# PEER's expert sums in a two-layer decoder trunk: v's rows as the moving operand, 512 channels at a time

## The chip, the cores and the metric

The kernel runs on one core of one Trainium2 chip. Its time is device microseconds (us) of one execution. The kernel before takes 2011.32 us, the median of three runs (2011.18 to 2011.91). The engines are TensorE (PE; its weight loads are listed as PEld), VectorE (DVE), ScalarE (ACT), GpSimd (POOL) and SyncE (SP, which issues the DMAs). All of them work side by side, each through its own instructions in order, and wait for one another by semaphores.

## The reference

Two layers of a decoder trunk work on 256 tokens of 1024 channels in float32. Each layer has a mixer (layer 0: mLSTM and block attention, layer 1: differential attention) and then PEER, a feed-forward part that retrieves experts:

```python
def peer_ffn(x, wq, keys, u, v):            # x: 256 tokens x 1024
    qry = (xt @ wq).reshape(t, PEER_HEADS, 2, PEER_DK // 2)
    sub = einsum('thpd,pnd->thpn', qry, keys)        # 8 heads, 2 x 128 sub-keys
    s_top, i_top = lax.top_k(sub, 16)
    ...                                              # 16 best of the 256 candidates
    idx, gate = ...                                  # out of 128 * 128 experts, softmax gates
    act = gelu(einsum('td,thkd->thk', x, u[idx])) * gate
    return einsum('thk,thkd->td', act, v[idx])       # added to x, times a gate of the layer
```

The last line is what the change is about: for every token a gated sum of rows of v, which has 16384 rows of 1024 channels.

## The kernel before

The kernel does not gather. It computes PEER densely: the 16384 experts are 128 tiles of 128. In the first half of `peer_body` it forms for each tile the 128 x 256 values gelu(u x) (`h_tile`) and multiplies them by a gate that is zero where the expert was not chosen (`gate_group`); the results stay in SBUF as A, 128 experts on the partitions by 256 tokens, 128 times. In the second half (the loop over `order`, lines 889 to 929) it sums A times v over all experts.

Products have float32 accuracy by splitting. Each operand is cast to a rounded part `hi` (float32r) and the rest `lo`; three matmuls, hi x hi, hi x lo and lo x hi, stand for one product. For a tile of v, `wsplit` has SP load 128 x 1024 floats (512 KB) into a ring of buffers `raw`, ACT cast it to `hi` (line 159) and DVE subtract to `lo` (line 162); `hi` and `lo` have three buffers each, so these two run up to three tiles ahead of PE. For each group of four tiles ACT and DVE split A in the same way into `act` (lines 904 and 905, two buffers, of the tag "x" in the pool `hp`). Beside it, `side` loads rows of the next modulation matrix, which DVE reduces (line 252): in layer 0, 8 steps over the first 64 tiles and 24 over the next 52; in layer 1, 8 late ones. From tile 64 on the ring `raw` is 15 buffers deep, before that 3.

The sums of the second half stand with channels on the partitions: `acc[dt]`, 128 channels by 256 tokens, for eight `dt`. A block of v (128 experts x 128 channels) is the stationary operand and A (128 experts x 256 tokens) the moving one, so a tile takes 8 x 3 matmuls of 256 columns. The eight sums lie in six PSUM banks: dt 0 to 3 share two of the tag "acc" in pairs, dt 4 and 5 have one each of that tag, and dt 6 and 7 one each of the tag "h". As two sums share a bank, the banks are first cleared by a matmul with zeros (line 891) and all matmuls add. At the last tile (the last three tiles are taken together, `batch`) each finished sum goes to `ffn_out`: DVE multiplies it by the gate and adds it to xT, the residual stream (line 935). In layer 0 `norm_stat` follows, where ACT squares and DVE adds for the next norm, and after the eighth PE sums over the partitions (line 290) with some matmuls of zeros around it (line 268); in layer 1 SP sends each 128 channels out (line 939).

Instructions are recorded in program order and then put in order for each engine by a scheduler that looks at dependences and priorities, so neighbours in the code can change places on an engine.

Another stage of the kernel has matmuls of 512 columns: `mm_row` (lines 237 to 239), in which the activations are stationary and 512 columns of a weight move, again in three products.

Of the kernel before, what the change touches and what calls it, by code (L numbers as in the profile page):

```python
# [9 lines left out]
F32 = mybir.dt.float32  # L10
# [10 lines left out]
P = 128  # L21
D = 1024
KD = D // P
T = 256
TT = T // P
EPS = 1e-6
NEG = -1e32
NEXP = 128
# [27 lines left out]
class Cols:  # L56
# [14 lines left out]
    c = 174  # L71
# [3 lines left out]
class Prog:  # L75
# [743 lines left out]
    def peer_body(self, layer, side, st):  # L819
        nc, tc = self.nc, self.tc  # L820
# [4 lines left out]
        hp = self.hp  # L825
# [11 lines left out]
        h = (hhi, hlo)  # L837
# [9 lines left out]
        for i, ps in self.col_tiles([self.io["wq"][layer, i] for i in range(16)], h, ("acc",) * 3, ws=ws):  # L847
            q = sp.tile([P, T], F32, tag="qry", name="qry", bufs=2)
# [14 lines left out]
        while live:  # L863
# [6 lines left out]
            with tc.issue_after(self.last_lo.ins):  # L870
                while credit > 0 and live:
                    c = next(topk, None)
# [7 lines left out]
        while i < NEXP:  # L880
# [5 lines left out]
                ohs = nxt  # L886
                done += G_TOK
            yield
        banks = [self.psum("acc") for _ in range(4)] + [self.psum("h") for _ in range(2)]
        for b in banks:  # L890
            nc.tensor.matmul(b, lhsT=self.zero.to_broadcast([P, P]), rhs=self.iota.unsqueeze(1).to_broadcast([P, 4, P]),
                             start=True, stop=False)
        acc = [banks[k // 2 if k < 4 else k - 2][:, k % 2 * T if k < 4 else 0:][:, :T] for k in range(KD)]
        order = list(range(64, 128)) + list(range(64))
        batch, nside = [], 0
        for n, e in enumerate(order):
            if n % 4 == 0:
                if n == 64:
                    a1p.__exit__(None, None, None)
                    late = st.enter_context(tc.tile_pool(name=f"late{layer}", bufs=1, reuse_waits="tile"))  # L900
                    self.raw_ring = (late, LATE_RING)
                x = hp.tile([P, 2, 4, T], F32, tag="x", name="act")
                src = A[e // 64][:, e % 64:e % 64 + 4, :]
                nc.scalar.copy(x[:, 0].bitcast(F32R), src)  # L904
                nc.vector.tensor_tensor(out=x[:, 1].bitcast(F32R), in0=src, in1=x[:, 0], op=ALU.subtract)  # L905
                xr = x.bitcast(F32R)
            vhi, vlo = self.wsplit(v[e])
            while nside < SIDE_N[layer][0] * min(n, 64) / 64 + SIDE_N[layer][1] * max(n - 64, 0) / SIDE_P2:
                next(side, None)
                nside += 1  # L910
            if n == NEXP - 8:
                for _ in side:
                    pass
            batch.append((n, vhi, vlo, xr))
            if n < NEXP - 3 or n == NEXP - 1:
                for dt in range(KD):
                    for m, vhi, vlo, xr in batch:
                        s = slice(dt * P, (dt + 1) * P)
                        xhi, xlo = xr[:, 0, m % 4, :], xr[:, 1, m % 4, :]
                        nc.tensor.matmul(acc[dt], lhsT=vhi[:, s], rhs=xhi, start=False, stop=False)  # L920
                        nc.tensor.matmul(acc[dt], lhsT=vhi[:, s], rhs=xlo, start=False, stop=False)  # L921
                        nc.tensor.matmul(acc[dt], lhsT=vlo[:, s], rhs=xhi, start=False, stop=m == NEXP - 1 and dt not in (0, 2))  # L922
                    if n == NEXP - 1 and dt not in (0, 2):
                        for d in (dt - 1, dt) if dt < 4 else (dt,):
                            self.ffn_out(layer, d, acc[d])
                batch = []
            yield
        self.raw_ring = self.stream_ring
        yield

    def ffn_out(self, layer, kd, y):

        nc = self.nc
        x = self.xT[:, kd, :]
        nc.vector.scalar_tensor_tensor(x, y, self.mod[:, layer, 40 + kd:41 + kd], x, op0=ALU.mult, op1=ALU.add)
        if layer == 0:
            self.norm_stat(kd)
        else:
            nc.sync.dma_start(self.out[:, kd, :], x)
# [263 lines left out]
```

## Time and profile before

| | |
|---|---|
| median of three runs | 2011.32 us |
| the profiled execution's own time | 2012.58 us |
| its span in the trace | 2010.8 us |
| PE busy | 1970.7 us (98%) |
| DVE, ACT busy | 1536.1 us (76%), 1131.6 us (56%) |
| second half of PEER, layer 0 | about 650 to 1020 us |
| second half of PEER, layer 1 | about 1636 to 2007 us |

All rows come from one profiled execution. A matmul's row gives its start and how long it was under way; matmuls overlap, so what one costs in a row of them is the distance between starts, not that duration. "PEclk" is the granted clock of TensorE as a share of its full 2.4 GHz. "DMA share" is the mean busy share of the core's 16 DMA engines. An idle time before an instruction is given in brackets with what ended it.

### The profile page before, as it was taken

Reading aid. Unit: us, or ns where it says so; the run is one execution under the profiler, and the core shown is the slowest. Engines: PE = TensorE matmul, PEld = TensorE weight load, DVE = VectorE, ACT = ScalarE, POOL = GpSimd, SP = SyncE. Lnnn points to the kernel's source line nnn. Section 1 sums busy time; section 2 is a strip of 40 time slices with the busy share of each in tenths; the row PEclk is TensorE's granted clock in tenths of the full one; section 3 lists DMA queues with packets and bytes.
Section 4 is the critical chain, followed back from the end, with each engine's and each line's share of the span. In section 5 each row is a group of like instructions: output and inputs, shape, how many; then the busy total and the mean of one; then the engine's idle time right before and its main releaser. Section 6 shows DMA issues by size and latency. Waiting matters only on the chain.

```text
span 2010.8 us, 41035 instructions
## 1 busy us (share of the span) xinstructions
PE 1970.7 (98%) x16281; PEld 1912.6 (95%) x16281; DVE 1536.1 (76%) x3328; ACT 1131.6 (56%) x2129; POOL 48.3 (2%) x37
## 2 busy tenths in 40 slices
PE   5999999999999999999999999999999999999999
PEld 4888999999999999999988799999999999999999
DVE  8887998788998555677578789988899955556554
ACT  4655555878775444444456554567877644444443
POOL 0020000000000000000012100000000000000000
PEclk9999999999999999999999999999999999999999
DMA  8863355444445666998266143554444455569650
GB/s 325 283 211 128 108 183 187 158 164 162 154 158 189 195 210 204 339 320 305 84 226 206 62 150 116 179 178 162 164 158 158 158 180 186 181 195 339 215 194 22
DMA packets 104016, 376.84 MB, mean 187 GB/s; under 512 B 11536, under 2 KB 12944, under 8 KB 103696
## 3 DMA queue, kind: packets, MB, share of 16 engines
q1 hardware_dynamic: 103824, 374.22, 55.1%
q8 instruction: 128, 2.10, 0.4%
q14 instruction: 64, 0.52, 0.1%
HBM read 373.12 MB, written 1.05 MB: 186 GB/s over the span
## 4 chain that ended last, share of the span: by engine, by line
PE 88%; issue 6%; DVE 3%; DMA 2%; ACT 1%; POOL 1%; POOLq 0%; ACTq 0%; DVEq 0%; SPq 0%
PE ps_h L185 14%; PE ps_h L187 14%; PE ps_h L186 14%; PE ps_acc L921 9%; PE ps_acc L922 9%; PE ps_acc L920 9%; PE ps_g L1094 3%; PE ps_h L922 3%; PE ps_h L921 3%; PE ps_h L920 3%; PE ps_l L389 1%; DVE lo L162 1%; DVE raw L252 1%; PE ps_acc L959 1%; DMA raw<-in_ev_in_dram 1%
## 5 line engine op out<-in xcount | busy, mean ns | idle before, releaser
L159 ACT CAST hi<-raw 128x1024 fp32r<-128x1024 f32 x613 | 641.4, 1047 | 701.4 <-PE ps_h L921 382.5
L162 DVE TENSOR_TENSOR lo<-raw,hi 128x1024 fp32r<-128x1024 f32 x613 | 748.3, 1221 | 342.7 <-ACT hi L159 342.4
L185 PE MATMUL ps_h<-h2hi,hi 128*128 128x256 f32 x2256 | 652.9, 289 | 0.5
L187 PE MATMUL ps_h<-h2hi,lo 128*128 128x256 f32 x2256 | 638.3, 283 | 0.0
L186 PE MATMUL ps_h<-h2lo,hi 128*128 128x256 f32 x2256 | 638.3, 283 | 0.0
L920 PE MATMUL ps_acc<-act,hi 128*128 128x256 f32 x1536 | 434.3, 283 | 0.7 <-ACT act L904 0.7
L921 PE MATMUL ps_acc<-act,hi 128*128 128x256 f32 x1536 | 434.4, 283 | 0.1
L922 PE MATMUL ps_acc<-act,lo 128*128 128x256 f32 x1536 | 433.9, 283 | 0.0
L185 PEld LDWEIGHTS ps_h<-h2hi,hi 128*128 128x128 f32 x2256 | 432.0, 191 | 1.9 <-ACT A L952 1.0
L186 PEld LDWEIGHTS ps_h<-h2lo,hi 128*128 128x128 f32 x2256 | 433.0, 192 | 0.0
L187 PEld LDWEIGHTS ps_h<-h2hi,lo 128*128 128x128 f32 x2256 | 432.3, 192 | 0.7
L920 PEld LDWEIGHTS ps_acc<-act,hi 128*128 128x128 f32 x1536 | 294.5, 192 | 2.0 <-ACT act L904 1.7
L921 PEld LDWEIGHTS ps_acc<-act,hi 128*128 128x128 f32 x1536 | 294.8, 192 | 0.5 <-DVE act L905 0.5
L922 PEld LDWEIGHTS ps_acc<-act,lo 128*128 128x128 f32 x1536 | 294.7, 192 | 0.0
L921 PE MATMUL ps_h<-act,hi 128*128 128x256 f32 x512 | 144.8, 283 | 0.0
L922 PE MATMUL ps_h<-act,lo 128*128 128x256 f32 x512 | 144.8, 283 | 0.0
L920 PE MATMUL ps_h<-act,hi 128*128 128x256 f32 x512 | 144.6, 283 | 0.0
L252 DVE CUSTOM_DVE_ANT_0 raw<-raw,crow,small 128x1024 f32<-128x1024 f32 x96 | 122.6, 1279 | 22.3 <-DMA raw<-in_ada_w_dram 21.9
L1101 DVE SCALAR_TENSOR_TENSOR A<-A,ps_g 128x256 f32<-128x256 f32 (+28 forms) x214 | 124.2, 581 | 11.9 <-PE ps_g L1094 11.0
L1103 ACT ACTIVATE A<-ps_g 128x256 f32<-128x256 f32 (+39 forms) x170 | 69.1, 445 | 76.9 <-DVE A L1101 75.8
L1081 DVE TENSOR_TENSOR og<-oj,gt 128x512 f16<-128x512 f16 x256 | 100.6, 419 | 13.3 <-PE ps_g L1094 13.1
L1068 ACT ACTIVATE oi<-iota,in 128x128 f16<-128x128 f16 x320 | 107.1, 394 | 0.0
(319 smaller groups left out, 2586.4 us busy)
## 6 DMA issues: line engine op xcount, KB each, us to landing
raw<-in_uT_dram SPq DMA_DIRECT2D x256, 512.0 KB, 3.3
raw<-in_v_dram SPq DMA_DIRECT2D x256, 512.0 KB, 4.3
raw<-in_ada_w_dram SPq DMA_DIRECT2D x96, 512.0 KB, 4.6
raw<-in_wq_dram SPq DMA_DIRECT2D x32, 512.0 KB, 4.6
raw<-in_ev_in_dram SPq DMA_DIRECT2D x21, 512.0 KB, 5.3
raw<-in_od_in_dram SPq DMA_DIRECT2D x16, 512.0 KB, 4.3
raw<-in_ev_v_dram SPq DMA_DIRECT2D x8, 512.0 KB, 5.3
raw<-in_ev_out_dram SPq DMA_DIRECT2D x8, 512.0 KB, 4.3
```

The lines of the kernel that those rows point to most:

```text
L159: nc.scalar.copy(hi, raw)
L162: self.last_lo = nc.vector.tensor_tensor(out=lo, in0=raw, in1=hi.bitcast(F32), op=ALU.subtract)
L185: nc.tensor.matmul(ps, lhsT=whi[:, s], rhs=ahi[:, kd, :], start=kd == kds[0], stop=False)
L186: nc.tensor.matmul(ps, lhsT=whi[:, s], rhs=alo[:, kd, :], start=False, stop=False)
L187: nc.tensor.matmul(ps, lhsT=wlo[:, s], rhs=ahi[:, kd, :], start=False, stop=kd == kds[-1])
L252: nc.vector.tensor_tensor_reduce(w, w, self.crow, 1.0, self.small[:, ab:ab + 1], ALU.mult, ALU.add, m)
L920: nc.tensor.matmul(acc[dt], lhsT=vhi[:, s], rhs=xhi, start=False, stop=False)
L921: nc.tensor.matmul(acc[dt], lhsT=vhi[:, s], rhs=xlo, start=False, stop=False)
L922: nc.tensor.matmul(acc[dt], lhsT=vlo[:, s], rhs=xhi, start=False, stop=m == NEXP - 1 and dt not in (0, 2))
L1068: nc.scalar.activation(oi[:, k, :], self.iota, AF.Square, bias=tabs["in"][:, t0 + k:t0 + k + 1])
L1081: nc.vector.tensor_tensor(out=og[:, w], in0=oj, in1=tabs["g"][:, w, ts].unsqueeze(1).to_broadcast(full), op=ALU.mult)
L1101: nc.vector.scalar_tensor_tensor(dst, dst, 1.0 / GSC, pv[:, :, lo:m], op0=ALU.mult, op1=ALU.mult)
```

## The change

The operands of the second half change places. `act` becomes the stationary operand, 128 experts by 128 tokens at a time, and v's rows the moving one, 128 experts by 512 channels. The sums stand with tokens on the partitions: four of them, `acc[q]`, two halves of the channels by two halves of the tokens, each of 128 x 512 and so one whole PSUM bank of the tag "acc". A tile takes 4 x 3 matmuls of 512 columns. The clearing by zeros is gone; the first matmul of each bank starts the sum. At the end of a layer each bank is copied to SBUF, 256 columns by ACT and 256 by DVE, into a new tile `y` of the tag "x"; PE transposes y in blocks of 128 x 128 (16 for a layer) into banks of the tag "h", two sums of 256 tokens to a bank, and `ffn_out`, which is the same as before, takes them from there.

```diff
--- before.py
+++ after.py
@@ -886,11 +886,7 @@
                 ohs = nxt
                 done += G_TOK
             yield
-        banks = [self.psum("acc") for _ in range(4)] + [self.psum("h") for _ in range(2)]
-        for b in banks:
-            nc.tensor.matmul(b, lhsT=self.zero.to_broadcast([P, P]), rhs=self.iota.unsqueeze(1).to_broadcast([P, 4, P]),
-                             start=True, stop=False)
-        acc = [banks[k // 2 if k < 4 else k - 2][:, k % 2 * T if k < 4 else 0:][:, :T] for k in range(KD)]
+        acc = [self.psum("acc") for _ in range(4)]
         order = list(range(64, 128)) + list(range(64))
         batch, nside = [], 0
         for n, e in enumerate(order):
@@ -913,20 +909,39 @@
                     pass
             batch.append((n, vhi, vlo, xr))
             if n < NEXP - 3 or n == NEXP - 1:
-                for dt in range(KD):
+                if n == NEXP - 1:
+                    y = hp.tile([P, TT, D], F32, tag="x", name="y")
+                for q in range(4):
+                    half, tt = q // 2, q % 2
+                    c, t = slice(512 * half, 512 * half + 512), slice(tt * P, (tt + 1) * P)
                     for m, vhi, vlo, xr in batch:
-                        s = slice(dt * P, (dt + 1) * P)
-                        xhi, xlo = xr[:, 0, m % 4, :], xr[:, 1, m % 4, :]
-                        nc.tensor.matmul(acc[dt], lhsT=vhi[:, s], rhs=xhi, start=False, stop=False)
-                        nc.tensor.matmul(acc[dt], lhsT=vhi[:, s], rhs=xlo, start=False, stop=False)
-                        nc.tensor.matmul(acc[dt], lhsT=vlo[:, s], rhs=xhi, start=False, stop=m == NEXP - 1 and dt not in (0, 2))
-                    if n == NEXP - 1 and dt not in (0, 2):
-                        for d in (dt - 1, dt) if dt < 4 else (dt,):
-                            self.ffn_out(layer, d, acc[d])
+                        xhi, xlo = xr[:, 0, m % 4, t], xr[:, 1, m % 4, t]
+                        nc.tensor.matmul(acc[q], lhsT=xhi, rhs=vhi[:, c], start=m == 0, stop=False)
+                        nc.tensor.matmul(acc[q], lhsT=xlo, rhs=vhi[:, c], start=False, stop=False)
+                        nc.tensor.matmul(acc[q], lhsT=xhi, rhs=vlo[:, c], start=False, stop=m == NEXP - 1)
+                    if n == NEXP - 1:
+                        for part, copy in ((0, nc.scalar.copy), (1, nc.vector.tensor_copy)):
+                            copy(y[:, tt, 512 * half + 256 * part:512 * half + 256 * part + 256],
+                                 acc[q][:, 256 * part:256 * part + 256])
+                        if q == 2:
+                            self.ffn_half(layer, y, 0)
+                        if q == 3:
+                            self.ffn_half(layer, y, 1)
                 batch = []
             yield
         self.raw_ring = self.stream_ring
         yield
+
+    def ffn_half(self, layer, y, half):
+
+        for two in range(2):
+            ps = self.psum("h")
+            for k in range(2):
+                kd = 4 * half + 2 * two + k
+                for tt in range(TT):
+                    o = k * T + tt * P
+                    self.nc.tensor.transpose(ps[:, o:o + P], y[:, tt, kd * P:(kd + 1) * P], self.ident)
+                self.ffn_out(layer, kd, ps[:, k * T:(k + 1) * T])
 
     def ffn_out(self, layer, kd, y):
 
```

PE where the second half of layer 0 begins. `ps_acc` and `ps_h` are the banks of the sums, `act` the split activations, `hi` and `lo` the split v, `zero` and `iota` the operands of the clearing. Before:

```order
L186 MATMUL ps_h<-h2lo,hi 128x256
L187 MATMUL ps_h<-h2hi,lo 128x256
L891 LDWEIGHTS zero
L891 MATMUL ps_acc<-iota,zero 128x512
L891 LDWEIGHTS zero
L891 MATMUL ps_acc<-iota,zero 128x512
L891 LDWEIGHTS zero
L891 MATMUL ps_h<-iota,zero 128x512
L920 MATMUL ps_acc<-act,hi 128x256 x3
L891 LDWEIGHTS zero
L891 MATMUL ps_h<-iota,zero 128x512
L920 MATMUL ps_acc<-act,hi 128x256
```

And now:

```order
L186 MATMUL ps_h<-h2lo,hi 128x256
L187 MATMUL ps_h<-h2hi,lo 128x256
L919 MATMUL ps_acc<-hi,act 128x512 x4
L920 MATMUL ps_acc<-hi,act 128x512
L921 MATMUL ps_acc<-lo,act 128x512
L920 MATMUL ps_acc<-hi,act 128x512
L921 MATMUL ps_acc<-lo,act 128x512
```

The clearing is gone, and the four hi x hi products of the first tile stand ahead of the first product that needs act's lo part (lines 920 of after). Two more clearing matmuls of each layer stood earlier in the order before, in the first half, and are gone too.

PE at the end of layer 0, from the third bank's last product (`y` is the copied sum, `ident` the identity of the transposes). Now:

```order
L921 MATMUL ps_acc<-lo,act 128x512
L943 MATMUL ps_h<-ident,y 128x128 x4
L919 MATMUL ps_acc<-hi,act 128x512
L920 MATMUL ps_acc<-hi,act 128x512
L943 MATMUL ps_h<-ident,y 128x128 x2
L921 MATMUL ps_acc<-lo,act 128x512
L919 MATMUL ps_acc<-hi,act 128x512
L920 MATMUL ps_acc<-hi,act 128x512
L943 MATMUL ps_h<-ident,y 128x128 x2
L921 MATMUL ps_acc<-lo,act 128x512
L919 MATMUL ps_acc<-hi,act 128x512
L920 MATMUL ps_acc<-hi,act 128x512
```

After one more product stand the eight transposes of the second half of the channels. The first eight are among the products of the fourth bank; before, the last product of dt 7 was followed by the matmuls of zeros of line 268.

DVE at the end of layer 0. `xT` is the residual stream, `sqsum` the squares for the next norm, `nv` the next norm's mean. Before:

```order
L935 SCALAR_TENSOR_TENSOR xT<-ps_acc,mod,xT 128x256
L281 TENSOR_TENSOR sqsum<-sqsum,sq 128x256
L935 SCALAR_TENSOR_TENSOR xT<-ps_h,mod,xT 128x256
L281 TENSOR_TENSOR sqsum<-sqsum,sq 128x256
L935 SCALAR_TENSOR_TENSOR xT<-ps_h,mod,xT 128x256
L281 TENSOR_TENSOR sqsum<-sqsum,sq 128x256
L299 TENSOR_SCALAR nv<-ps_g 128x2
```

And now:

```order
L924 COPY y<-ps_acc 128x256 x2
L950 SCALAR_TENSOR_TENSOR xT<-ps_h,mod,xT 128x256
L924 COPY y<-ps_acc 128x256
L950 SCALAR_TENSOR_TENSOR xT<-ps_h,mod,xT 128x256 x3
L281 TENSOR_TENSOR sqsum<-sqsum,sq 128x256 x3
L924 COPY y<-ps_acc 128x256
L950 SCALAR_TENSOR_TENSOR xT<-ps_h,mod,xT 128x256 x3
L281 TENSOR_TENSOR sqsum<-sqsum,sq 128x256
L950 SCALAR_TENSOR_TENSOR xT<-ps_h,mod,xT 128x256
L281 TENSOR_TENSOR sqsum<-sqsum,sq 128x256 x2
L299 TENSOR_SCALAR nv<-ps_g 128x2
```

The last copy stands behind three additions of squares, and four of the eight gated additions to xT stand behind it. In the rest of the program the engines keep their order but for some of DVE's side reductions and three loads of the next mixer's weights, which SP now issues up to eight loads of v later.

## Rows read from the trace of the kernel before

**Rows 1.** Page, part 1: busy time, share of the span, instructions of each engine.

```profile
PE 1970.7 (98%) x16281; PEld 1912.6 (95%) x16281; DVE 1536.1 (76%) x3328; ACT 1131.6 (56%) x2129; POOL 48.3 (2%) x37
```

**Rows 2.** Page, part 4: shares of the chain that ended last, by engine.

```profile
PE 88%; issue 6%; DVE 3%; DMA 2%; ACT 1%; POOL 1%; POOLq 0%; ACTq 0%; DVEq 0%; SPq 0%
```

**Rows 3.** Stretches: from:to, length, busy of PE, PEld, DVE, ACT, POOL, clock, DMA.

```profile
652.40:1013.00 360.60, 360.60 (x3004) 360.46 (x3005) 226.51 (x228) 160.20 (x156) 0.34 (x1) 1.00 0.68 234
1637.00:2000.00 363.00, 362.61 (x3017) 362.19 (x3018) 199.98 (x175) 161.81 (x159) 0.00 (x0) 1.00 0.57 192
```

**Rows 4.** Timeline (start, us under way), PE, products of 256 columns in layer 0.

```profile
985.05 0.28 PE L920 MATMUL ps_h<-act,hi 128*128 128x256 f32 x1
...
987.93 0.28 PE L920 MATMUL ps_h<-act,hi 128*128 128x256 f32 x1
```

**Rows 5.** Timeline, PE, products of 512 columns in the stage of mm_row.

```profile
65.18 0.40 PE L237 MATMUL ps_h<-hi,hhi 128*128 128x512 f32 x1
...
67.70 0.39 PE L239 MATMUL ps_h<-hi,hlo 128*128 128x512 f32 x1
...
78.94 0.39 PE L239 MATMUL ps_h<-hi,hlo 128*128 128x512 f32 x1
...
87.10 0.39 PE L239 MATMUL ps_h<-hi,hlo 128*128 128x512 f32 x1
```

**Rows 6.** Timeline, PE, five matmuls of zeros (float16, 512 columns), merged.

```profile
1022.56 1.24 PE L268 MATMUL ps_h<-iota,zero 128*128 128x512 f16 x5
```

**Rows 7.** Timeline where layer 0's second half begins.

```profile
649.96 1.04 ACT L904 CAST act<-A 128x1024 fp32r<-128x1024 f32 x1 [1.55 <-PE ps_h L186]
...
651.06 0.62 PE L920 MATMUL ps_acc<-act,hi 128*128 128x256 f32 x3 [0.35 <-ACT act L904]
652.32 0.39 PE L921 MATMUL ps_acc<-act,hi 128*128 128x256 f32 x1
```

**Rows 8.** Waits in layer 0's second half: total us, times, longest.

```profile
ACT hi L159 <- PE ps_h L921: 182.2, 115, 1.8
...
ACT hi L159 <- DMA raw<-in_v_dram: 18.0, 10, 3.0
```

**Rows 9.** Stretches of layer 0's second half with the most transfers; columns as in rows 3.

```profile
830.00:850.00 20.00, 20.00 (x169) 20.00 (x168) 16.44 (x20) 9.25 (x9) 0.00 (x0) 1.00 1.03 409
890.00:910.00 20.00, 20.00 (x169) 20.00 (x168) 15.81 (x21) 9.23 (x9) 0.00 (x0) 1.00 0.86 294
```

**Rows 10.** Groups: copies out of PSUM, 256 and 258 columns, count, busy, mean ns.

```profile
L742 ACT COPY z<-ps_h 128x256 f32<-128x256 f32 x15 | 5.4, 365 | 2.2 <-PE ps_h L187 2.2
L667 DVE COPY mnum<-ps_l 128x258 f32<-128x258 f32 x4 | 1.6, 421 | 0.8 <-PE ps_l L666 0.8
```

**Rows 11.** Timeline: three transposes merged; three gated additions merged.

```profile
90.47 0.49 PE L621 MATMUL ps_t<-ident,qk 128*128 128x128 f32 x3
2003.10 1.27 DVE L935 SCALAR_TENSOR_TENSOR xT<-ps_acc,mod,xT 128x256 f32<-128x256 f32 x3 [0.33 <-PE ps_acc L922]
```

**Rows 12.** Timeline at the end of layer 0.

```profile
1020.46 0.28 PE L922 MATMUL ps_h<-act,lo 128*128 128x256 f32 x1
1020.77 0.48 DVE L935 SCALAR_TENSOR_TENSOR xT<-ps_h,mod,xT 128x256 f32<-128x256 f32 x1 [0.23 <-PE ps_h L922]
1021.17 0.41 DVE L281 TENSOR_TENSOR sqsum<-sqsum,sq 128x256 f32<-128x256 f32 x1
1021.64 0.38 PE L290 MATMUL ps_g<-ones,sqsum 128*128 128x1 f32 x2 [0.24 <-DVE sqsum L281]
```

**Rows 13.** Timeline at the end of layer 1.

```profile
2006.73 0.28 PE L922 MATMUL ps_h<-act,lo 128*128 128x256 f32 x1
2007.05 0.48 DVE L935 SCALAR_TENSOR_TENSOR xT<-ps_h,mod,xT 128x256 f32<-128x256 f32 x1 [0.59 <-PE ps_h L922]
```

**Rows 14.** Stretches around a fall of the clock early on; columns as in rows 3.

```profile
38.00:40.00 2.00, 0.74 (x4) 0.54 (x4) 2.00 (x5) 0.40 (x1) 0.00 (x0) 0.90 1.01 406
42.00:44.00 2.00, 2.00 (x11) 2.00 (x11) 0.89 (x3) 1.13 (x2) 0.00 (x0) 0.50 1.01 399
```

## The prediction

> **What bounds the kernel now.** The busy shares come first: PE is busy 98% of the span and DVE, the next, 76% [rows 1]. A busy share alone says little, so the chain of waits is read next: 88% of the chain that ended last is PE's own work [rows 2]. The view by stretches then shows the two halves that the change touches: over 360.6 us of layer 0 and 363 us of layer 1 PE has no idle time worth a name, at a granted clock of 1.00, with DVE busy 63% and 55% and ACT 44% and 45% [rows 3]. The view of waits says the same from the other side: ACT waits 115 times, 182.2 us in all, for PE to give a buffer of the split v back, and only 10 times for a load [rows 8]. So a tile of v costs what PE's 24 matmuls cost, and DVE, ACT and the loads follow.
>
> **What one tile costs, before and after.** Matmuls overlap, so the reader is to measure from start to start. A product of 256 columns is under way 0.28 us, but the first product of one tile starts at 985.05 and its like in the next at 987.93: 24 products in 2.88 us, 0.1200 us each [rows 4]; the long stretch confirms it, with 3004 products in 360.6 us [rows 3]. For products of 512 columns of the same type, with weights as moving and activations as stationary operand, the kernel has mm_row. Its fast run of 37 products, with no other work between, takes 8.16 us from the first start to the last, 36 distances of 0.2267 us; a run of 12 takes 2.52 us, 11 distances of 0.2291 us [rows 5]. Two products of 256 columns take 0.2400 us, one of 512 takes 0.2267. At the full 2.4 GHz, 256 columns are 106.7 ns and 512 are 213.3 ns, so each product carries some 13.3 ns beside its columns in both widths; the change moves the same columns in half as many products. I take 0.2267, from the longer run and so the nearer to a loop without pauses, and keep 0.2291 for the upper end.
>
> A tile: 24 x 0.1200 = 2.880 us before, 12 x 0.2267 = 2.720 after, 0.160 less. Two layers of 128 tiles: 256 x 0.160 = **41.0 us less**.
>
> **Does anything else become late at 2.72 us a tile?** In layer 0 DVE is busy 1.81 us a tile and ACT 1.28 (226.5 and 160.2 of 360.6 us, times 2.88) [rows 3]; the busiest stretch has DVE at 16.44 us of 20 [rows 9], which at 6% more pace is 17.4 of 20. The loads run at 409 GB/s with a DMA share of 1.03 while the ring of 15 is being filled, and at 294 GB/s with 0.86 once it is full [rows 9]. At the new pace the second becomes 311 GB/s at 0.91. The filling runs as fast as the DMA engines can and is ahead of need. Ten waits of ACT for loads, the longest 3.0 us [rows 8], cost PE nothing before: the three buffers of hi and lo hold PE's work of two tiles beside the one on hand, 5.76 us before and 5.44 now. So I cost the feed at nothing; its cover is those two tiles. SP's later issue of three loads for the next mixer costs nothing either: they still come ahead of the last loads of v, which the ring of 15 takes some 40 us before PE needs them.
>
> **The start of the half.** Before, PE got the first hi part at 651.06 and the lo part at 652.32, and did six products of 256 columns between [rows 7], worth 0.72 us of what follows. Now four products of 512 stand there, 0.91 us, which fit the 1.26 us: 0.19 us less in each layer, 0.4 us in all. Of the twelve clearing matmuls, eight stood where PE waits for act in any case, and four stood in the busy first half; five such follow each other in 1.24 us [rows 6], about 0.215 us each, so their going gives 0.9 us.
>
> **The end of the half.** This is what the change adds, 16 transposes, 8 copies and a longer last step for each layer.
> - Eight transposes stand among the products of the fourth bank. Three take 0.49 us with 0.27 us for one alone, so 0.11 us each [rows 11]: 0.9 us a layer, 1.8 us in all, on PE's path.
> - Layer 1. Before, the last product starts at 2006.73, its slot of 0.12 ends at 2006.85, DVE's gated addition runs from 2007.05 to 2007.53 [rows 13]: 0.68 us behind the slot. Now, counted from the slot's end: 0.20 until the bank can be read, a copy of 0.37 on ACT and 0.42 on DVE side by side [rows 10], 0.1 for the hand-over, two transposes until the first addition can start (0.11 + 0.27, and 0.05 for the wait), then four additions, of which three take 1.27 us [rows 11], 0.40 apart: 0.20 + 0.37 + 0.05 + 0.43 = 1.05, + 3 x 0.40 + 0.48 = 2.73 us. That is 2.1 us more. The other transposes go on beside the additions.
> - Layer 0. Before, PE's slot ends at 1020.58 and the sum over partitions starts at 1021.64, 1.06 us later [rows 12]. Now the last copy on DVE stands behind three additions of squares. With the additions to xT 0.40 us apart and those of squares 0.33, DVE gets to it some 0.4 us after the bank is ready; the copy ends 1.0 us behind the slot, four additions to xT and four of squares fill about 2.7 us more: 3.7 us in all, 2.7 us more than before. ACT's squares lie beside them. Behind the waiting copy nothing is queued that PE needs sooner, since all that follows is this chain.
>
> The ends together: 1.8 + 2.1 + 2.7 = 6.6 us more. From below this could be 3 us, if the scheduler's copies and additions overlap better than I have them, and from above 9 us, if each hand-over costs 0.3 us and the last four outputs, now close together, queue behind each other.
>
> **Sum.** -41.0 - 0.4 - 0.9 + 6.6 = -35.7 us. Against the profiled execution's own 2012.58 us this is 1976.9. The median of the runs shown is 1.26 us below that execution, so on the runs' scale it is 2011.3 - 35.7 = **1975.6 us**.
>
> **A rule against the change.** In the rows, a product of 256 columns costs 13.3 ns more than its columns [rows 4]. The Trainium skill (TensorE: Matmul & The Clock Gate, section Back-to-back issue gap) gives the distance of two matmuls at full clock as the columns at 2.4 GHz plus about 2.5 ns. The float16 products of rows 6 are near that; those of the second half are not: the page gives 109 ns where the trace has 120. By the page's figures a tile would go from 2.62 to 2.59 us, an estimate of 8 us saved in all, little more than the ends cost. The rows decide, as both widths stand in them in the same number type.
>
> **Rivals.**
> 1. The 13 ns do not belong to the product but grow with its columns or come with the stationary operand, which now changes at every product where mm_row kept it for two of three. Then 512 columns take 0.240 us in the new loop, a tile stays at 2.88 us, and what is left is the ends less the start: +6.6 - 1.3 = +5.3, **2016.6 us**, slower. It decides from a distance of 0.2400 - 5.3/3072 = 0.2383 us on. For it: only 192 products of this width stand in the trace, in two stages, and the new pattern in none. Against it: none of the long runs is over 0.2291, and the changes of the stationary operand in mm_row show no longer step. By the page's rule above the time would stand just inside this rival's near end, about 2009 us. Chance 4% for slower, 2% for a time within 0.2%.
> 2. The feed binds in layer 0's stretch of side work: about 42 tiles between 830 and 950 us stay at 2.88 us and lose 42 x 0.16 = 6.7 us: **1982 us**. For it, a DMA share of 1.03 [rows 9]; against it, the ring of 15 and the drop to 0.86 afterwards. Chance 6%.
> 3. The clock falls in the longer pause at layer 0's end. Early in the span, after 2 us with PE busy 0.74, the granted clock went from 0.90 to 0.50, the lower level of 1.2 GHz, and PE did 11 products in 2 us [rows 14] where it does 16.7 at full clock [rows 3]. Six microseconds of dense work at that pace would lose 6 x (1 - 11/16.7) = 2 us: **1978 us**. Against it: the transposes and the matmuls of zeros stand in the pause. No gap of PE in my sum is longer than 1.3 us. Chance 7%.
> 4. The products come closer together than in mm_row, toward the 0.215 us of rows 6: each ns under 0.2267 gives 3.1 us, so 0.225 would give **1970 us**. Chance 5%.
>
> The forecast itself has 76%. Its own range is 1972 to 1983 (0.2267 to 0.2291 is 7.4 us; the ends 3 to 9 us); with rivals 2 to 4 in it the range is **1970 to 1985 us**. A change under 0.2%, 4 us, can't be told from none. Faster 0.94, same 0.02, slower 0.04.
>
> **What would show it.** In the profile of the changed kernel: lines 919 to 921 with 3072 products in all and starts 0.227 us apart; casts of v on ACT 2.72 us apart in place of 2.88; the waits of ACT still for PE; a span of layer 0's half of about 348 us; between the last product's slot and line 290 about 3.7 us in place of 1.1. The prediction is wrong if the distance is 0.235 or more, if PE waits for hi or lo in the middle of the half, or if the ends take over 10 us together.

## The result, and the profile after

The changed kernel took 1980.38 us (median of 4 runs, 1977.66 to 1983.62) where the kernel before took 2011.25 beside it: ratio 0.9848, 95% interval 0.9831 to 0.9865. Timed again in a later series it took 1977.47 (5 runs, 1975.56 to 1978.42) against 2011.80: 0.9828, 0.9815 to 0.9841. The forecast of 1975.6 is 2 to 5 us below, and both medians lie in its range of 1970 to 1985.

The page of the changed kernel gives busy times by engine, and by line the busy time, the mean ns of one instruction, and the idle time in front:

```profile
PE 1934.8 (98%) x13229; PEld 1754.6 (89%) x13229; DVE 1538.6 (78%) x3336; ACT 1136.1 (57%) x2137; POOL 50.7 (3%) x37
...
L919 PE MATMUL ps_acc<-hi,act 128*128 128x512 f32 x1024 | 397.8, 389 | 2.0 <-ACT act L900 2.0
L920 PE MATMUL ps_acc<-hi,act 128*128 128x512 f32 x1024 | 398.6, 389 | 0.1
L921 PE MATMUL ps_acc<-lo,act 128*128 128x512 f32 x1024 | 398.6, 390 | 0.0
```

PE does 3052 fewer instructions and is still busy 98%, as in [rows 1]. The three lines of the new loop wait for nothing but the half's start. The view of stretches has the distances (columns as in [rows 3]); here the changed kernel inside layer 0's half:

```profile
660.00:980.00 320.00, 320.00 (x1413) 265.00 (x1412) 216.04 (x218) 152.38 (x148) 0.34 (x1) 1.00 0.74 253
```

320.00 / 1413 = 0.2265 us a product, against 0.1200 for half the columns in [rows 3, 4]. A stretch also counts the products that straddle its edges, so the starts are the finer measure. These are the first products of two tiles, 80 tiles apart:

```profile
703.04 0.39 PE L919 MATMUL ps_acc<-hi,act 128*128 128x512 f32 x1
...
920.64 0.39 PE L919 MATMUL ps_acc<-hi,act 128*128 128x512 f32 x1
```

217.60 us for 960 products are 0.2267 us each and 2.720 us a tile, as in the forecast. The waits of layer 0's half, in the form of [rows 8] (what waited and for what, total, times, longest):

```profile
ACT hi L159 <- PE ps_acc L920: 129.2, 92, 1.7
...
ACT hi L159 <- DMA raw<-in_v_dram: 44.0, 27, 3.0
```

ACT still waits mostly for PE. It now waits for a load 27 times instead of 10, and none of that reaches PE.

At layer 0's end the timeline shows what took the place of [rows 12]. First PE:

```profile
997.83 0.39 PE L921 MATMUL ps_acc<-lo,act 128*128 128x512 f32 x1
998.06 0.38 PE L943 MATMUL ps_h<-ident,y 128*128 128x128 f32 x2
998.91 0.33 PE L943 MATMUL ps_h<-ident,y 128*128 128x128 f32 x1 [0.47 <-ACT y L924]
999.59 1.34 PE L943 MATMUL ps_h<-ident,y 128*128 128x128 f32 x5 [0.36 <-DVE y L924]
1001.00 0.81 PE L268 MATMUL ps_h<-iota,zero 128*128 128x512 f16 x3
1002.58 0.61 PE L290 MATMUL ps_g<-ones,sqsum 128*128 128x1 f32 x4 [0.78 <-DVE sqsum L281]
...
1003.80 2.29 PE L268 MATMUL ps_h<-iota,zero 128*128 128x512 f16 x5
```

and ACT and DVE beside it:

```profile
998.50 0.35 ACT L924 COPY y<-ps_acc 128x256 f32<-128x256 f32 x1
```

```profile
991.92 0.42 DVE L924 COPY y<-ps_acc 128x256 f32<-128x256 f32 x1 [0.93 <-ACT y L924]
...
997.73 1.47 DVE L281 TENSOR_TENSOR sqsum<-sqsum,sq 128x256 f32<-128x256 f32 x3
999.12 0.42 DVE L924 COPY y<-ps_acc 128x256 f32<-128x256 f32 x1
999.46 1.49 DVE L950 SCALAR_TENSOR_TENSOR xT<-ps_h,mod,xT 128x256 f32<-128x256 f32 x3
1000.86 0.41 DVE L281 TENSOR_TENSOR sqsum<-sqsum,sq 128x256 f32<-128x256 f32 x1
1001.19 0.48 DVE L950 SCALAR_TENSOR_TENSOR xT<-ps_h,mod,xT 128x256 f32<-128x256 f32 x1
1001.59 0.94 DVE L281 TENSOR_TENSOR sqsum<-sqsum,sq 128x256 f32<-128x256 f32 x2
```

The last product's slot ends at 998.06 and the sum over partitions starts at 1002.58: 4.52 us, where it was 1.06. The copy of 991.92 names ACT's copy as what it waited for: the two copies of one bank follow each other. The last DVE copy is held longer still, by three additions of squares that stand in front of it. From 999.12 to 1002.5 DVE has no gap at all. And the five matmuls of zeros behind the sums take 2.29 us, against 1.24 in [rows 6]: the clock has fallen. The stretches there say when:

```profile
1000.00:1002.00 2.00, 1.67 (x7) 0.64 (x7) 1.98 (x5) 1.14 (x3) 0.00 (x0) 1.00 0.00 0
1002.00:1004.00 2.00, 1.42 (x9) 1.33 (x10) 0.45 (x2) 1.97 (x3) 0.00 (x0) 0.80 0.00 0
1004.00:1012.00 8.00, 6.89 (x25) 4.96 (x24) 6.09 (x13) 3.34 (x7) 1.62 (x1) 0.50 0.26 81
```

Layer 1 ends like this, where [rows 13] has one addition:

```profile
1969.32 0.39 PE L921 MATMUL ps_acc<-lo,act 128*128 128x512 f32 x1
...
1969.75 0.37 ACT L924 COPY y<-ps_acc 128x256 f32<-128x256 f32 x1 [2.71 <-PE ps_acc L921]
1970.15 0.42 DVE L924 COPY y<-ps_acc 128x256 f32<-128x256 f32 x1 [0.85 <-ACT y L924]
...
1970.54 1.96 DVE L950 SCALAR_TENSOR_TENSOR xT<-ps_h,mod,xT 128x256 f32<-128x256 f32 x4
...
1971.08 0.20 PEld L943 LDWEIGHTS ps_h<-ident,y 128*128 128x128 f32 x2 [0.31 <-DVE xT L950]
1971.54 0.20 PEld L943 LDWEIGHTS ps_h<-ident,y 128*128 128x128 f32 x2 [0.26 <-DVE xT L950]
```

The last four transposes (PEld: their weight loads) wait for additions to xT: two sums lie in a bank of the tag "h", and the second is written there only when the addition has read the first. So the four additions take 1.96 us, where 0.40 us apart they would take 1.68.

From the slot's end at 1969.55 to the end of the span at 1975.9 are 6.35 us, before 3.95 (2006.85 to 2010.8).

Cut at the same events, the spans of the profiled executions divide as follows (us; "again" is the changed kernel profiled a second time, in the later series).

| from ... to | before | changed | again |
|---|---|---|---|
| span's start to layer 0's PEER, line 306 | 189.32 | 186.64 | 187.47 |
| to the first cast of act, layer 0 | 460.64 | 460.42 | 461.53 |
| layer 0's second half, to the last slot's end | 370.62 | 351.00 | 351.04 |
| to the sum, line 290 | 1.06 | 4.52 | 4.52 |
| to line 306 of mixer 1 | 3.19 | 3.51 | 3.20 |
| to line 306 of layer 1's PEER | 150.63 | 151.79 | 150.75 |
| to the first cast of act, layer 1 | 460.78 | 460.66 | 460.77 |
| layer 1's second half | 370.61 | 351.01 | 351.02 |
| to the span's end | 3.95 | 6.35 | 6.30 |
| span | 2010.8 | 1975.9 | 1976.6 |

The stages that the change edits give, in "again" less before, -19.58 + 3.46 - 19.59 + 2.35 = -33.4 us. What else differs lies in stages with the same instructions, and there the granted clock differs: the early fall of [rows 14] lies at another time in each execution. Stretches of the changed kernel's first trace:

```profile
8.00:16.00 8.00, 0.00 (x0) 0.00 (x0) 8.00 (x20) 2.08 (x5) 0.00 (x0) 0.62 1.03 415
...
32.00:40.00 8.00, 6.52 (x33) 5.73 (x31) 8.00 (x16) 4.11 (x7) 0.00 (x0) 0.67 1.01 385
```

and of its second:

```profile
32.00:40.00 8.00, 5.54 (x32) 4.39 (x31) 8.00 (x16) 3.70 (x6) 0.00 (x0) 1.00 0.97 359
40.00:48.00 8.00, 7.81 (x51) 7.61 (x52) 5.66 (x10) 5.55 (x10) 0.00 (x0) 0.79 0.79 284
```

In the first the clock is low from about 10 to 37 us; in the second it falls between 40 and 48, near the place of [rows 14].

### The profile page after: what moved, and what is told of

The parts are those of the page before. It is cut to its first block, busy times and chain, and to the rows that moved or that the text cites. A ratio compares the mean times of both kernels' runs of the same rounds, so it can differ in the third digit from the quotient of the medians.

```text
span 1975.9 us, 34938 instructions
## 1 busy us (share of the span) xinstructions
PE 1934.8 (98%) x13229; PEld 1754.6 (89%) x13229; DVE 1538.6 (78%) x3336; ACT 1136.1 (57%) x2137; POOL 50.7 (3%) x37
## 3 DMA queue, kind: packets, MB, share of 16 engines
HBM read 373.12 MB, written 1.05 MB: 189 GB/s over the span
## 4 chain that ended last, share of the span: by engine, by line
PE 79%; DVE 12%; issue 5%; DMA 2%; ACT 1%; POOL 0%; POOLq 0%; ACTq 0%; DVEq 0%; SPq 0%
PE ps_h L185 12%; PE ps_acc L920 12%; PE ps_acc L921 12%; PE ps_acc L919 12%; PE ps_h L186 11%; PE ps_h L187 11%; DVE lo L162 4%; PE ps_g L1109 3%; DVE raw L252 1%; DMA raw<-in_ada_w_dram 1%; PE ps_l L389 1%; DVE idxs L987 1%; DVE mr L985 1%; DVE A L1116 1%; DVE idxs L984 1%
## 5 line engine op out<-in xcount | busy, mean ns | idle before, releaser
L919 PE MATMUL ps_acc<-hi,act 128*128 128x512 f32 x1024 | 397.8, 389 | 2.0 <-ACT act L900 2.0
L920 PE MATMUL ps_acc<-hi,act 128*128 128x512 f32 x1024 | 398.6, 389 | 0.1
L921 PE MATMUL ps_acc<-lo,act 128*128 128x512 f32 x1024 | 398.6, 390 | 0.0
L919 PEld LDWEIGHTS ps_acc<-hi,act 128*128 128x128 f32 x1024 | 192.1, 188 | 41.8 <-ACT act L900 2.4
L920 PEld LDWEIGHTS ps_acc<-hi,act 128*128 128x128 f32 x1024 | 192.2, 188 | 40.8 <-DVE act L901 1.0
L921 PEld LDWEIGHTS ps_acc<-lo,act 128*128 128x128 f32 x1024 | 192.0, 188 | 40.5 <-DVE lo L162 0.3
L185 PE MATMUL ps_h<-hhi,hi 128*128 128x256 f32 x248 | 76.0, 308 | 7.4 <-ACT hhi L449 3.4
L1109 PE MATMUL ps_g<-oi,og 128*128 128x128 f16 x1024 | 81.8, 223 | 0.0
L901 DVE TENSOR_TENSOR act<-A,act 128x1024 fp32r<-128x1024 f32 x64 | 78.0, 1218 | 1.5 <-ACT act L900 1.5
```

Of the source, the lines that this page charges most:

```text
L185: nc.tensor.matmul(ps, lhsT=whi[:, s], rhs=ahi[:, kd, :], start=kd == kds[0], stop=False)
L919: nc.tensor.matmul(acc[q], lhsT=xhi, rhs=vhi[:, c], start=m == 0, stop=False)
L920: nc.tensor.matmul(acc[q], lhsT=xlo, rhs=vhi[:, c], start=False, stop=False)
L921: nc.tensor.matmul(acc[q], lhsT=xhi, rhs=vlo[:, c], start=False, stop=m == NEXP - 1)
L1109: nc.tensor.matmul(pv[:, k, :], lhsT=og[:, w, :, k], rhs=oi[:, k, :], start=w == 0, stop=w == 1)
```

## The experiments

Theory: a product of this type costs its columns' time and a fixed 13 ns, whatever the roles of its operands, and half as many products save 41 us; the longer ends and a fall of the clock behind layer 0 give some back. Rivals: the exchanged operands save the time; the 13 ns belong to a change of the stationary operand; the miss against the forecast lies in the loop and not at the ends.

### e1_half_width: the new roles at the old width

```
+        for b in acc:
+            nc.tensor.matmul(b, lhsT=self.zero.to_broadcast([P, P]), rhs=self.iota.unsqueeze(1).to_broadcast([P, 4, P]),
+                             start=True, stop=False)
...
-                        nc.tensor.matmul(acc[q], lhsT=xhi, rhs=vhi[:, c], start=m == 0, stop=False)
...
+                    for w in range(2):
+                        cw, aw = slice(512 * half + 256 * w, 512 * half + 256 * w + 256), acc[q][:, 256 * w:256 * w + 256]
...
+                            nc.tensor.matmul(aw, lhsT=xhi, rhs=vhi[:, cw], start=False, stop=False)
```

The two other products change in the same way. As two sums share a bank again, the clearing by zeros is back too, four matmuls a layer.

> The changed loop keeps its operands' roles (act stationary, v's rows streamed) but each product streams 256 channels, so 24 products per expert again, two sums to a bank. Theory (a product takes its columns' time plus a fixed 13 ns, whatever the roles): products 0.120 us apart, +0.160 us per expert, 256 experts, so the whole +41 us of the changed kernel comes back: about 2021 us, ratio to before about 1.005. Rival (the exchange of the operands is what gains, the width does not matter): about 1980 to 1985 us, ratio 0.985 to 0.987.

Measured: 2021.01 us (4 runs), ratio 1.0049 [1.0033, 1.0064]. The whole gain is gone. Its stretch in layer 0:

```profile
660.00:980.00 320.00, 320.00 (x2669) 320.00 (x2668) 206.45 (x210) 142.85 (x139) 0.00 (x0) 1.00 0.73 254
```

320 / 2669 = 0.1199 us: the distance of [rows 4] with the roles exchanged. Each half takes 371.83 us, 20.8 more than in the changed kernel; 128 x 0.160 is 20.5, and the rest stands at the start of the half, where the clearing is. So the gain comes with the width, that is with half as many products and weight loads for the same columns; the exchange alone only brings the costlier ends.

### e2_same_operand: one product in three has the stationary operand of the one before it

```
                         nc.tensor.matmul(acc[q], lhsT=xhi, rhs=vhi[:, c], start=m == 0, stop=False)
-                        nc.tensor.matmul(acc[q], lhsT=xlo, rhs=vhi[:, c], start=False, stop=False)
-                        nc.tensor.matmul(acc[q], lhsT=xhi, rhs=vlo[:, c], start=False, stop=m == NEXP - 1)
+                        nc.tensor.matmul(acc[q], lhsT=xhi, rhs=vlo[:, c], start=False, stop=False)
+                        nc.tensor.matmul(acc[q], lhsT=xlo, rhs=vhi[:, c], start=False, stop=m == NEXP - 1)
```

> The three products of an expert in another order: act-hi by v-hi, act-hi by v-lo, act-lo by v-hi, so that one product in three keeps the stationary operand of the one before it. Theory (the 13 ns belong to every product): distance stays 0.2264 us, time as the changed kernel, about 1980 us within 2. Rival (the 13 ns are the price of another stationary operand): one product in three at 0.2133, 1024 of them by 0.0133 less: about 13.5 us less, 1967 us.

Measured: 1977.73 us (5 runs), ratio 0.9834 [0.9820, 0.9847], between the two timings of the changed kernel. In the timeline, lines 919 and 920 have act-hi as the stationary operand, line 921 has act-lo:

```profile
900.90 0.39 PE L920 MATMUL ps_acc<-lo,act 128*128 128x512 f32 x1
901.13 0.39 PE L921 MATMUL ps_acc<-hi,act 128*128 128x512 f32 x1
901.35 0.39 PE L919 MATMUL ps_acc<-hi,act 128*128 128x512 f32 x1
901.58 0.39 PE L920 MATMUL ps_acc<-lo,act 128*128 128x512 f32 x1
```

The three steps are 0.23, 0.22 and 0.23; the one from line 919 to 920, with the same operand, is no shorter. The long stretch and the weight loads of line 920 say more:

```profile
660.00:980.00 320.00, 320.00 (x1413) 265.06 (x1412) 215.47 (x218) 153.62 (x148) 0.34 (x1) 1.00 0.74 253
```

```profile
L920 PEld LDWEIGHTS ps_acc<-lo,act 128*128 128x128 f32 x1024 | 192.3, 188 | 40.0 <-DVE lo L162 0.5
```

The count in 320 us is that of the changed kernel, so the rival falls as it was put: another stationary operand costs no more than the same one. But line 920 has 1024 weight loads for 1024 products, so the same operand is loaded again each time. Whether a product without a load would be rid of the 13 ns was not run, and what the 13 ns are is not known from these runs.

### e3_no_ends: the price of the ends

```
-                        for part, copy in ((0, nc.scalar.copy), (1, nc.vector.tensor_copy)):
...
-                            self.ffn_half(layer, y, 0)
...
-                            self.ffn_half(layer, y, 1)
+                        for k in range(2):
+                            self.ffn_out(layer, 2 * q + k, acc[q][:, k * T:(k + 1) * T])
```

> Leaves out the copies and transposes at each layer's end: the residual update takes the banks as they are (so channels and tokens are mixed up in the output; the amount of the other work is the same). Theory (the ends cost what the two traces show): layer 0 end 4.5 -> about 1.5 us, layer 1 end 6.35 -> about 4.4, 16 transposes in line -1.8, the clock holds behind layer 0: -1.2; sum about -8, 1972.5 us. Rival (ends cost no more than my forecast's 6.6 us, and the rest of the miss sits in the loop): 1975 us or more, with the loop's 128 experts over 350 us as in the changed kernel less the transposes.

Measured: 1970.22 us (5 runs), ratio 0.9801 [0.9788, 0.9815]. By its trace the halves take 349.97 and 349.94 us, the pause to line 290 is 1.71 and the end 4.60: 1.0 + 1.1 + 2.8 + 1.75 = 6.7 us less than the changed kernel, at the same distance (1414 products in 320.00 us). The 6.7 us lie near the rival's 6.6, but the ends of e3 are themselves 1.3 us longer than before (1.71 and 4.60 against 1.06 and 3.95), so the ends of the change cost 7.9 to 8.0 us. The halves, 20.65 and 20.67 us shorter than before, have what the forecast gave the loop. The miss against the forecast that the traces show is thus at the ends, as the theory had it. The expected hold of the clock failed: it falls here too, to 0.63 in the stretch from 1000 to 1002 us and 0.50 behind it, after a pause shorter than the changed kernel's.

### e4_warm: more zero products at layer 0's end

```
                         if q == 3:
+                            if layer == 0:
+                                self.keep_warm(6)
                             self.ffn_half(layer, y, 1)
 ...
-            self.norm_stat(kd)
+            self.norm_stat(kd, (6, 8))
```

> At the end of layer 0 of the changed kernel 6 more zero products ahead of the last 8 transposes, and 6 and 8 in place of 3 and 5 around the sums of squares. Theory (the granted clock falls to 0.5 behind the pause, and that costs): clock 1.00 from layer 0's end on, 1.2 us less, some 1979 us, and less spread between runs. Rival A (the fall follows from what lay earlier): 0.5 stays, 1980.4 us. Rival B (the zero products stand in the way): +0.5 to +1.5 us, 1981 to 1982.

Measured: 1979.53 us (5 runs), ratio 0.9843 [0.9830, 0.9857]. The mechanism is there in the trace, the gain in time is not. Stretches behind the end:

```profile
999.00:1001.00 2.00, 2.00 (x12) 0.99 (x10) 1.54 (x5) 0.68 (x2) 0.00 (x0) 1.00 0.00 0
1001.00:1003.00 2.00, 1.51 (x8) 0.75 (x8) 1.86 (x6) 1.01 (x3) 0.00 (x0) 1.00 0.00 0
...
1007.00:1009.00 2.00, 0.73 (x5) 0.55 (x5) 1.10 (x3) 0.58 (x2) 0.10 (x1) 1.00 0.70 231
```

The clock holds at 1.00 through the pause and the start of mixer 1. But line 290 comes 0.35 us later (4.87 behind the slot), and in this execution the clock falls once later, in the stretch from 1117 to 1127 (0.83), and the way from line 290 to layer 1's PEER is 155.40 us, no shorter than the 155.30 of the changed kernel's first trace. A microsecond is below what five runs tell here: inconclusive in time.

### after_again, e5_short_ends and e6_short_warm: can the ends be shortened?

All three ran on the same chip. e5 moves the first half's transposes one tile of the last batch (three products) earlier, does four transposes of the last half ahead of the last bank's last three products, and gives both last copies to ACT; e6 adds zero products. The batch has three tiles, so the edit moves them half as far as the two experts and six products that were expected of it.

```
+                        if n == NEXP - 1 and b == 2:       # after two of the batch's three tiles
+                            if q == 2:
+                                self.ffn_half(layer, y, 0)
+                            if q == 3:
+                                self.ffn_half(layer, y, 1, (0,))   # token half 0 alone
 ...
-                        for part, copy in ((0, nc.scalar.copy), (1, nc.vector.tensor_copy)):
+                        for part, copy in ((0, nc.scalar.copy), (1, nc.scalar.copy if q == 3 else nc.vector.tensor_copy)):
 ...
+                            if layer == 0:                 # e6 alone
+                                with tc.issue_after(mm.ins):
+                                    self.keep_warm(3, "g")
+            self.norm_stat(kd, (6, 8))                     # e6 alone
```

> The changed kernel as it is, beside the two that shorten its ends. Theory (the stretches in which the granted clock falls to 0.5 change from run to run: the start, and sparse stretches of mixer 1): 1980.4 us within 1, and clock stretches that need not be those of the first trace. Rival (they belong to the program): the same stretches again, 9 to 37 us and 1003 to 1013 us.

> The changed kernel with the first half's transposes two experts earlier, the four transposes of the last half that need only bank 2 ahead of the last bank's last six products, and the last bank's two copies both on ACT. Theory (at the ends VectorE is what everything waits for: its copy behind ACT's, then four updates and the adds): pause at layer 0's end 4.5 -> 3.5 to 4.0 us, at layer 1's end 6.35 -> 5.5 to 6.0; sum -1 to -1.8, 1979 us. Rival (the copy's place is hidden, the updates are late anyway): no change in the two pauses, 1980.4.

> The same, with 3 zero products between the last bank's last product and its transposes, and 6 and 8 in place of 3 and 5 around the sums of squares at layer 0's end. Theory: the clock holds at 1.00 behind layer 0's end, as in e4_warm, 1.2 us less than e5_short_ends in the stage behind, at the price of up to 0.4 us at the sums: 1978 us. Rival (zero products gain nothing net): 1979 to 1980.

Measured: 1977.47, 1978.52 and 1978.05 us (5 runs each); ratios 0.9828, 0.9834 and 0.9834, each within 0.0013. No difference.

The trace of e5 says where its gain went. The pause to line 290 is 4.03 us in place of 4.52, a smaller gain than the theory gave, and layer 1's end is 6.3 us in both, as the rival had it. The first update of xT does start earlier behind the slot, 1.00 us in place of 1.40. But each half takes 0.4 us longer (351.47 and 351.45), since four transposes that left the ends now stand between the products:

```profile
998.47 0.39 PE L926 MATMUL ps_acc<-lo,act 128*128 128x512 f32 x1
998.70 0.60 PE L947 MATMUL ps_h<-ident,y 128*128 128x128 f32 x4
999.05 0.48 PE L924 MATMUL ps_acc<-hi,act 128*128 128x512 f32 x1
999.37 0.39 PE L925 MATMUL ps_acc<-hi,act 128*128 128x512 f32 x1
```

From 998.47 to 999.37 two products go by that take 0.45 without the four transposes: 0.45 us for the group, 0.11 each, as in [rows 11]. In layer 0 the two cancel; in layer 1 nothing stands against them.

In e6 the clock holds, as in e4, and here the whole way from line 290 to layer 1's PEER is back at 153.83 us (before: 153.82), where e5, with its fall, has 155.35. The pause is 4.02 us, so the zero products cost nothing there. What they are worth is less sure: the second trace of the changed kernel has no added zero products and a later, shorter fall, and its way is 153.95. So by these traces they gain between 0.1 and 1.5 us, depending on when the clock would have fallen; the medians, half a microsecond apart, don't resolve it.

The second trace of the changed kernel decides against the rival of after_again: the early fall lies between 40 and 48 us and not at 10 to 37, and the one behind layer 0 begins near 1010 us, 10 us behind the slot, where it was 5 in the first.

### e7_two_products: how much room the feed has

```
-                        nc.tensor.matmul(acc[q], lhsT=xlo, rhs=vhi[:, c], start=False, stop=False)
```

> Leaves out the product of act-lo and v-hi (so the output lacks that correction): 8 products an expert in place of 12, 1.81 us in place of 2.72. Theory (loads, casts and splits have room at 2.72 us): 256 experts by 0.906 us less, 232 us, some 1748 to 1760 us. Rival (the feed is nearly as long: DMA share 0.74 in layer 0's stretch with the side transfers): it stops at about 2.0 us an expert in layer 0 and 1.8 in layer 1, 1775 us or more.

Measured: 1831.61 us (2 runs), ratio 0.9106 [0.9089, 0.9122]: 146 us less than the changed kernel's 1977.47 and not 232. The theory is wrong, and the larger loss is not where the rival looked. Stretches in layer 0's first 64 tiles and in its side work, and early and late in layer 1:

```profile
660.00:780.00 120.00, 106.56 (x391) 70.39 (x390) 79.46 (x73) 61.83 (x60) 0.00 (x0) 0.97 0.75 236
820.00:860.00 40.00, 37.09 (x149) 26.65 (x147) 37.94 (x46) 22.80 (x24) 0.00 (x0) 1.00 1.03 408
1562.00:1700.00 138.00, 127.30 (x494) 87.68 (x495) 92.75 (x79) 79.63 (x79) 0.00 (x0) 1.00 0.72 235
1700.00:1800.00 100.00, 98.72 (x432) 80.27 (x431) 88.31 (x84) 68.47 (x68) 0.00 (x0) 1.00 0.97 369
```

Lines 919 and 920 do 8 products a tile: 2.46 us a tile in the first stretch, 2.15 in the second, 2.23 in the third and 1.85 in the last, where eight products at 0.2267 us are 1.81. In the side work of layer 0, where the rival looked for the limit, the feed does hold PE, with DVE busy 37.94 of 40 us and a DMA share of 1.03; but ahead of it the pace is slower still. That first stretch has a DMA share of 0.75 with 1.03 to be had [rows 9], and its waits and loads are:

```profile
ACT hi L159 <- DMA raw<-in_v_dram: 50.9, 38, 3.3
```

```profile
raw<-in_v_dram SPq DMA_DIRECT2D x48, 512.0 KB, 4.3
raw<-in_ada_w_dram SPq DMA_DIRECT2D x6, 512.0 KB, 4.4
```

In the first 64 tiles of a half all loads go through three buffers, those of the side work too (`in_ada_w`). A buffer is held while a load lands (4.3 us from issue, by this row) and while cast and split read it (1.05 and 1.22 us each by the page): 6.6 us, an estimate of 2.2 us a load with three. The rows come out near it: 54 loads in 120 us, 2.2 us each, and in layer 1, where only one load of 65 in 138 us is side work, 2.1. So the side loads explain why a tile takes longer in layer 0. Where the ring has 15 buffers and little side work, the tile takes 1.85. That the three buffers are the cause is argued from these rows; a deeper ring in that stretch was not tried.

## Why the prediction was right, and what was mis-sized

| step, both layers | forecast | measured | from |
|---|---|---|---|
| distance of the products and the start | -41.4 | -41.3 | halves of e3 less before |
| clearing matmuls gone | -0.9 | not resolved | 460.78 before, 460.66 and 460.77 after, layer 1 |
| transposes among the products | +1.8 | +2.1 | halves of the changed kernel less e3 |
| layer 0's pause | +2.7 | +3.46 | the table of spans |
| layer 1's end | +2.1 | +2.40, 2.35 | the table of spans |
| sum | -35.7 | -33.4 | |

The clearing matmuls that were to give 0.9 us stood in the first halves, and that stage, from line 306 of layer 1's PEER on, takes 460.2 to 461.2 us in the traces of this loop, so a gain of 0.4 us a layer can't be told there.

**The distance.** Right in mechanism and size: 0.2267, as forecast. e1 shows the width as the cause, and neither rival 1's 0.2400 nor rival 4's closer products came. e2 adds that another stationary operand costs no more than the same one loaded again; whether the 13 ns come with the load stays open. The rule of the Trainium skill (TensorE: Matmul & The Clock Gate, section Back-to-back issue gap) that the prediction quotes, for 8 us saved, is not what these products do.

**The feed.** Costed at nothing, and nothing it cost: PE waits for no load, and 320 us of layer 0's busiest half are without a gap. Rival 2 did not come. The cover was named too generously, though: the prediction spoke of the two tiles in the buffers behind the split, while e7 shows a pace of 2.46 us a tile as the limit in layer 0's first 64 tiles. At 2.72 that leaves 0.26 us a tile.

**The ends.** The mis-sized term: 6.6 us forecast, 7.9 to 8.0 measured. In layer 1 the prediction had the four last additions 0.40 us apart and said that "the other transposes go on beside the additions". They don't: the last four wait for additions that read the same banks, and the additions come 0.49 us apart. The last one ends 2.95 us behind the slot and not 2.73, although the first starts at 0.99, a little ahead of the 1.05 of the forecast. In layer 0 the three additions of squares ahead of the last copy were in the forecast, but 0.33 us apart; one behind the other they take 1.47 us in place of 1.07, and the copy ends 1.48 us behind the slot and not 1.0. Behind it four additions to xT and three of squares (the forecast counted four) take 3.0 us and not 2.7.

The prediction also put the two copies of a bank "side by side" on ACT and DVE. The trace has them one behind the other, DVE's with ACT's copy as the one it waited for, though neither end is longer by that: in layer 1 the first addition is on time all the same, and in layer 0 the squares hold DVE's copy longer. The Trainium skill (PSUM — Partial Sum Buffer, section PSUM bank collisions raise a hardware error) says that two engines must not work on one bank at the same time and that accesses are to be ordered by bank. The order of the copies and that of the transposes agree, and the prediction should have weighed that rule; no run here tells the bank from the tile y, which both copies write, as the reason of the copies' order.

**The clock.** Rival 3 had 7% and came to pass in the first trace: 1.48 us more from line 290 to layer 1's PEER, of the 2 us that it gave. In the second trace it cost 0.13. It was no step of the sum, and the prediction's argument against it, that no gap of PE is over 1.3 us, held (the longest wait of PE there is 1.11 us) and did not help.

The remaining distance between the two medians, 1980.4 and 1977.5, is no larger than that between executions: at the start alone the two traces differ by 0.8 us, and the four runs of the first spread over 6 us.

## What to carry to other kernels

Where matmuls follow each other without a gap, measure the distance at two widths in the same number type before you count columns: here 13 ns a product stood beside them, and halving the number of products was worth 41 us without one column less. Price the ends by the serial engine that closes them, bank by bank, and ask what is queued ahead of the last copy and what waits for a bank to be read; work taken out of a pause into a loop without gaps is paid there at full price. Before going faster again, take one operation away to see where the feed stands: here its room was 10% in layer 0's first 64 tiles, where a DMA share of 0.74 and a DVE busy 68% suggest a quarter or more.

## What the runs showed of the hardware that was not expected

The granted clock falls behind layer 0's end in every trace of this loop without added zero products, and in neither of the two with them. PE's busy time in us in five stretches of 2 us, from the last whole microsecond ahead of the last slot's end on (1020, 998, 1000, 996, 999 and 998 us), and what the clock did:

```
before          1.75 1.80 0.71 1.33 1.69   held at 1.00
changed         1.11 1.67 1.42 2.00 1.31   0.80 in the third, then 0.50
changed, again  1.11 1.64 1.44 0.96 0.89   0.97 in the fifth, then 0.50
e3_no_ends      0.46 1.92 1.04 0.89 2.00   0.63 in the third, then 0.50
e4_warm         2.00 1.51 1.86 1.76 0.73   held at 1.00
e6_short_warm   1.79 1.66 1.87 1.60 0.88   held at 1.00
```

The two traces of the changed kernel do nearly the same work in the first two stretches, and in one the clock falls 5 us earlier than in the other. 0.50 is the lower of the two levels, 1.2 GHz. Weight loads show a second thing: at 256 columns they are under way without a break (320.00 of 320 us in e1), at 512 columns for 265 us of 320.
